# Half-row matmuls of the gate stage, side by side on the two halves of the array

## The chip, the cores and the metric

The kernel runs on one core of a Trainium2 chip. The metric is the device time of one launch in microseconds (us). The kernel before was run three times: 3077.47 us is the median, 3076.24 and 3080.39 us are the ends.

## The reference

Two layers on 2048 tokens of width 1024, then a final norm: an mLSTM layer, and a gated linear recurrence (RG-LRU). The change lies in the last stage, which does the second half of the RG-LRU layer. What is computed there:

```python
xc = causal_dwconv(xr, conv_w, conv_b)                      # 1536 channels
xb = xc.reshape(bsz, s, R_BLOCKS, R_BS)                     # 8 blocks of 192 channels
r  = sigmoid(einsum('bsnc,ncd->bsnd', xb, w_a).reshape(bsz, s, R_WIDTH) + b_a)
ig = sigmoid(einsum('bsnc,ncd->bsnd', xb, w_x).reshape(bsz, s, R_WIDTH) + b_x)
log_a = -LRU_C * r * softplus(-lam)
a  = exp(log_a)
bt = sqrt(-expm1(2.0 * log_a)) * (ig * xc)
hs = linear_scan(a, bt)                                     # h_t = a_t h_(t-1) + bt_t
y  = (hs * silu(g)) @ w_out                                 # 1536 -> 1024
x  = rmsnorm(x + y, final_g)
```

The two einsums are the gates: each is block diagonal, with blocks of 192 by 192.

## The kernel before, in words

The last stage is `phase_b2`. Channels lie on the 128 partitions, tokens on the free axis. Tokens go in four blocks `b` of 512, channels of the recurrence in four groups `p` of 384 = three tiles of 128 rows, which hold two of the 192-blocks: block one is tile 0 and rows 0 to 63 of tile 1, block two is rows 64 to 127 of tile 1 and tile 2. For each `b`, `p` and each of the two gates `j` (0 is `r`, 1 is `ig`), `gates` computes three output tiles `to`. Output tile 0 takes input tiles 0 and 1, output tile 1 takes 0, 1 and 2, output tile 2 takes 1 and 2: seven products. The weights are laid out as seven blocks of 128 by 128 in that order, with zeros where a product needs only half of the rows of tile 1 (the second and the sixth block).

Every product is done three times by `mm3` (lines 362 to 364): operands are split into a high part and a rest (`xch`, `xcl`, `wh`, `wl`; cast by ACT in line 735, rest by DVE in line 738), and high by high, high by rest and rest by high are summed in a bank of PSUM. So one gate of one group is 21 matmuls of 128 rows and 512 columns; there are 32 such sets. ACT then reads each bank: tanh, exp, tanh for `j` = 0 (lines 1298 to 1300, into `R` and `A`), one tanh for `j` = 1 (line 1302, into `ig`). A square root of `R` follows (line 1304), then the products and scans on DVE (lines 1307 to 1316), which give `yh` and `yl`.

`x2_out` multiplies these with the output weights (`acc`, 36 matmuls per step), adds the residual, and does the final norm (`ssum`, `srow`, `x2`, output). A list `steps` interleaves: one gate step, then, from the sixth gate step on, three steps of `x2_out` that lag five gate steps behind. The weights are fetched in that order, at most three ahead (`weights`, line 1242 for raw ones, which are split on the core; in block 0 the gates' split weights are also stored to DRAM, and blocks 1 to 3 load them back, line 1239). The order of instructions on each engine is made by a list scheduler from priorities and estimated times, so a change of one engine's order can change that of the others.

PE is TensorE; PEld are its weight loads, which have rows of their own in the trace; DVE, ACT, SP are VectorE, ScalarE, SyncE.

Of the kernel before, what the change touches and what calls it, by code (L numbers as in the profile page):

```python
# [14 lines left out]
P = 128  # L15
# [273 lines left out]
class Trunk:  # L289
# [923 lines left out]
    def phase_b2(self, rgate, rwout, D, outT):  # L1213


        tc, nc = self.tc, self.nc
        NT = 12
        with ExitStack() as ctx:
# [31 lines left out]
            def weights():  # L1250

                with tc.high_priority():
                    while order and len(ready) < 3:
                        ready.append(fetch(*order.pop(0)))
                return ready.pop(0)

            def psum(name):
                return pm.tile([P, TB], F32, tag="mm", name=name)

            def col(i, t):  # L1260
                return self.lc[:, i * NT + t:i * NT + t + 1]
# [19 lines left out]
            def gates(b, p, xs, ys):  # L1281

                R = tp.tile([P, 3, TB], F32, tag="R", name="R")
                A = tp.tile([P, 3, TB], F32, tag="A", name="A")
                G = tp.tile([P, 3, TB], F32, tag="ig", name="ig", bufs=1)
                xc, xh, xl = xs
                for j in range(2):
                    wh, wl = weights()
                    i = 0
                    for to, tis in ((0, (0, 1)), (1, (0, 1, 2)), (2, (1, 2))):  # L1290
                        ps = psum("gate")
                        for ti in tis:
                            ws = slice(i * P, (i + 1) * P)
                            self.mm3(ps, wh[:, ws], wl[:, ws], xh[:, ti], xl[:, ti], ti == tis[0], ti == tis[-1])
                            i += 1
                        t = p * 3 + to
                        if j == 0:
                            nc.scalar.activation(R[:, to], ps, AF.Tanh, scale=0.5, bias=col(2, t))
                            nc.scalar.activation(A[:, to], R[:, to], AF.Exp, scale=col(0, t), bias=col(0, t))
                            nc.scalar.activation(R[:, to], R[:, to], AF.Tanh, scale=col(1, t), bias=col(1, t))  # L1300
                        else:
                            nc.scalar.activation(G[:, to], ps, AF.Tanh, scale=0.5, bias=col(3, t))
                    if j == 0:
                        nc.scalar.activation(R, R, AF.Sqrt, scale=-0.25)
                        g = tp.tile([P, 3, TB], F32, tag="g", name="g")
                        nc.sync.dma_start(g, D["g"][p * 3:p * 3 + 3, :, b * TB:(b + 1) * TB].rearrange("k p t -> p k t"))
                        nc.vector.scalar_tensor_tensor(R, A, 1.0, R, op0=ALU.add, op1=ALU.mult)
                        yield
                nc.vector.scalar_tensor_tensor(xc, G, 1.0, xc, op0=ALU.add, op1=ALU.mult)
                nc.vector.tensor_tensor(R, R, xc, op=ALU.mult)  # L1310
                for to in range(3):
                    t = p * 3 + to
                    nc.vector.tensor_tensor_scan(xc[:, to], A[:, to], R[:, to], hc[:, t:t + 1], op0=ALU.mult,
                                                 op1=ALU.add)
                nc.gpsimd.tensor_copy(hc[:, p * 3:p * 3 + 3], xc[:, :, TB - 1])
                nc.vector.tensor_tensor(g, xc, g, op=ALU.mult)
                hi = tp.tile([P, 3, TB], F32R, tag="yh", name="yh", bufs=4)
                lo = tp.tile([P, 3, TB], F32R, tag="yl", name="yl", bufs=4)
                self.split_into(hi, lo, g, "a", "v")
                ys += [(hi[:, to], lo[:, to]) for to in range(3)]  # L1320
                yield

            def block(b):

                ys = blocks[b] = []
                if b == 0:
                    with tc.high_priority():
                        xs = load(b, 0)
                else:
                    xs = load(b, 0)  # L1330
                for p in range(4):
                    nxt = load(b, p + 1) if p < 3 else None
                    yield from gates(b, p, xs, ys)
                    xs = nxt
# [158 lines left out]
```

## Time and profile before

| | |
|---|---|
| median of 3 runs | 3077.47 us (3076.24 to 3080.39) |
| profiled execution | 3070.89 us, of which the span is 3069.1 us |
| PE busy | 2935.0 us, 96% |
| DVE, ACT busy | 2129.9 us (69%), 1460.0 us (48%) |
| last stage | from about 2584 us to the end |

The span runs from the first to the last instruction; what lies around it is 1.8 us. A matmul's row in the trace gives a time from start to end, but matmuls are pipelined: what one costs in a dense stream is the distance from its start to the next start, not its length.

### The profile page before, as it was taken

What the parts mean: (1) busy time and instruction counts of PE and PEld (TensorE: products, weight loads), DVE (VectorE), ACT (ScalarE), POOL (GpSimd) and SP (SyncE); (2) the same over time, 40 slices, a digit from 0 to 9 for tenths busy, and PEclk for the clock granted to TensorE, in tenths of its full rate; (3) what the DMA queues carried; (4) which work ended last, traced back from release to release, by engine and by line L of the source; (5) the groups of instructions that cost most, each with busy time, mean ns of one, the idle gap of its engine ahead of it and who ended that gap; (6) DMA issues with size and microseconds to landing.
All of it is one profiled execution on the core that took longest, in us unless ns stands there. A gap on an engine that the chain in (4) does not pass through costs nothing.

```text
span 3069.1 us, 43651 instructions
## 1 busy us (share of the span) xinstructions
PE 2935.0 (96%) x15730; PEld 2511.8 (82%) x15730; DVE 2129.9 (69%) x3825; ACT 1460.0 (48%) x2386; POOL 381.3 (12%) x407
## 2 busy tenths in 40 slices
PE   6999999999999899999999899999999998899997
PEld 4799987899988898989989777877888886687786
DVE  7866789534566587777778655687779375887775
ACT  5444546323434555555555322343445233877772
POOL 0111110000000234343333100000110000110100
PEclk9999999999999999999999899999999998999999
DMA  6766677666777645354534565666666666757743
GB/s 217 254 216 232 231 249 247 201 201 208 218 227 231 185 129 164 121 166 127 159 121 124 189 189 169 188 197 214 219 216 223 213 192 215 252 184 240 239 135 127
DMA packets 308986, 600.64 MB, mean 196 GB/s; under 512 B 27808, under 2 KB 106400, under 8 KB 308768
## 3 DMA queue, kind: packets, MB, share of 16 engines
q1 hardware_dynamic: 222784, 389.79, 41.6%
q10 hardware_dynamic: 59184, 107.77, 10.0%
q0 software_dynamic: 26800, 100.28, 8.4%
q8 instruction: 124, 2.03, 0.3%
q14 instruction: 94, 0.77, 0.1%
HBM read 388.86 MB, written 208.86 MB: 195 GB/s over the span
## 4 chain that ended last, share of the span: by engine, by line
PE 85%; DVE 6%; DMA 5%; ACT 2%; issue 1%; POOL 0%; SPq 0%; ACTq 0%; DVEq 0%; POOLq 0%
PE acc L362 6%; PE acc L363 6%; PE acc L364 6%; PE pj L362 3%; PE pj L363 3%; PE pj L364 3%; PE pd L362 3%; PE pc L362 3%; PE pd L363 3%; PE pd L364 3%; PE pc L364 3%; PE pc L363 3%; PE pa L362 3%; PE pa L363 3%; PE pa L364 3%; PE pb L363 2%
## 5 line engine op out<-in xcount | busy, mean ns | idle before, releaser
L735 ACT CAST s<-raw 128x512 fp32r<-128x512 f32 (+1 forms) x360 | 222.2, 621 | 500.9 <-PE acc L364 193.4
L738 DVE TENSOR_TENSOR s<-raw,s 128x512 fp32r<-128x512 f32 (+1 forms) x360 | 246.6, 688 | 91.5 <-ACT s L735 87.2
L362 PE MATMUL acc<-yh,s 128*128 128x512 f32 x512 | 204.5, 402 | 9.9 <-DVE x L1125 3.6
L363 PE MATMUL acc<-yl,s 128*128 128x512 f32 x512 | 203.9, 398 | 0.3 <-DVE yl L738 0.3
L364 PE MATMUL acc<-yh,s 128*128 128x512 f32 x512 | 202.8, 396 | 0.0
L362 PE MATMUL acc<-yh,wh 128*128 128x512 f32 x384 | 149.7, 397 | 13.5 <-ACT yh L735 8.9
L735 ACT CAST Ch<-C 128x516 fp32r<-128x516 f32 x120 | 74.8, 623 | 171.1 <-DVE da L944 120.1
L364 PE MATMUL acc<-yh,wl 128*128 128x512 f32 x384 | 150.9, 395 | 1.1 <-DVE wl L738 1.1
L363 PE MATMUL acc<-yl,wh 128*128 128x512 f32 x384 | 151.0, 394 | 0.3 <-DVE yl L738 0.2
L662 DVE SCALAR_TENSOR_TENSOR xc<-xm,vec,xc 128x512 f32<-128x512 f32 x192 | 140.3, 746 | 14.5 <-ACT xc L660 13.4
L735 ACT CAST s<-sum 128x512 fp32r<-128x512 f32 (+1 forms) x120 | 74.3, 620 | 146.7 <-PE pa L364 43.6
L738 DVE TENSOR_TENSOR Cl<-C,Ch 128x516 fp32r<-128x516 f32 x120 | 116.7, 972 | 20.9 <-ACT Ch L735 20.7
L362 PEld LDWEIGHTS acc<-yh,s 128*128 128x128 f32 x512 | 97.8, 191 | 35.7 <-DVE x L1125 4.5
L364 PEld LDWEIGHTS acc<-yh,s 128*128 128x128 f32 x512 | 97.3, 190 | 23.2 <-DVE s L738 0.3
L363 PEld LDWEIGHTS acc<-yl,s 128*128 128x128 f32 x512 | 97.3, 190 | 22.9 <-DVE yl L738 0.8
L735 ACT CAST wh<-wr 128x512 fp32r<-128x512 f32 (+1 forms) x104 | 65.4, 641 | 102.1 <-PE acc L363 63.6
L662 DVE SCALAR_TENSOR_TENSOR xc<-xr,vec,xc 128x512 f32<-128x512 f32 x144 | 104.8, 747 | 7.3 <-ACT xc L660 6.0
L738 DVE TENSOR_TENSOR s<-sum,s 128x512 fp32r<-128x512 f32 (+1 forms) x120 | 82.4, 688 | 39.2 <-ACT s L735 38.1
L738 DVE TENSOR_TENSOR wl<-wr,wh 128x512 fp32r<-128x512 f32 (+1 forms) x104 | 73.4, 716 | 51.7 <-ACT wh L735 51.2
L362 PE MATMUL gate<-xch,wh 128*128 128x512 f32 x224 | 92.7, 415 | 16.7 <-ACT xch L735 8.8
L362 PE MATMUL pj<-vwh,xmh 128*128 128x512 f32 x256 | 103.4, 404 | 0.0
L364 PE MATMUL pj<-vwh,xml 128*128 128x512 f32 x256 | 100.5, 392 | 0.0
(419 smaller groups left out, 9684.9 us busy)
## 6 DMA issues: line engine op xcount, KB each, us to landing
d_wx<-s POOLq DMA_DIRECT2D x64, 512.0 KB, 4.1
s<-d_wx SPq DMA_DIRECT2D x64, 512.0 KB, 4.4
raw<-in_wout_dram SPq DMA_DIRECT2D x128, 256.0 KB, 3.1
raw<-in_wxz_dram SPq DMA_DIRECT2D x124, 256.0 KB, 4.5
d_wr<-s POOLq DMA_DIRECT2D x48, 512.0 KB, 3.4
s<-d_wr SPq DMA_DIRECT2D x48, 512.0 KB, 4.4
wr<-in_rwout_dram SPq DMA_DIRECT2D x96, 256.0 KB, 2.9
raw<-in_rwin_dram SPq DMA_DIRECT2D x84, 256.0 KB, 3.8
```

What stands on the lines that cost most here:

```text
L362: mm(out, sh, mh, start=first, stop=False, skip_group_check=resumed)
L363: mm(out, sh, ml, start=False, stop=False, skip_group_check=resumed)
L364: mm(out, sl, mh, start=False, stop=last, skip_group_check=resumed)
L662: nc.vector.scalar_tensor_tensor(out, x[:, j:j + TB], self.v(wn, m * 4 + j), out, op0=ALU.mult, op1=ALU.add)
L735: a = nc.scalar.copy(hi, src)
L738: b = (nc.gpsimd if lo_eng == "p" else nc.vector).tensor_tensor(lo, src, hi.bitcast(F32), op=ALU.subtract)
```

## The change

Two of the seven products, output tile 0 with input tile 1 and output tile 2 with input tile 1, are issued on the 64 rows that are not zero: rows 0 to 63 for the one, rows 64 to 127 for the other. Their three parts are issued in turn, one for each of the two banks: six matmuls of 64 rows and 512 columns. For this the two banks are opened first with the whole products of tiles 0 and 2, and output tile 1 comes last, in matmuls as before. ACT reads the banks in the order 0, 2, 1. The number of matmuls per set stays 21.

```diff
-                    i = 0
-                    for to, tis in ((0, (0, 1)), (1, (0, 1, 2)), (2, (1, 2))):
-                        ps = psum("gate")
+                    pss = {}
+
+                    def full(to, tis, n, first, last):
                         for ti in tis:
-                            ws = slice(i * P, (i + 1) * P)
-                            self.mm3(ps, wh[:, ws], wl[:, ws], xh[:, ti], xl[:, ti], ti == tis[0], ti == tis[-1])
-                            i += 1
+                            ws = slice(n * P, (n + 1) * P)
+                            self.mm3(pss[to], wh[:, ws], wl[:, ws], xh[:, ti], xl[:, ti], first and ti == tis[0],
+                                     last and ti == tis[-1])
+                            n += 1
+                    for to, n in ((0, 0), (2, 6)):
+                        pss[to] = psum("gate")
+                        full(to, (to,), n, True, False)
+
+                    ends = ((0, slice(0, 64), slice(P, 2 * P)), (2, slice(64, P), slice(5 * P, 6 * P)))
+                    for st, mv in ((wh, xh), (wh, xl), (wl, xh)):
+                        for to, rs, ws in ends:
+                            nc.tensor.matmul(pss[to], st[rs, ws], mv[rs, 1], start=False, stop=st is wl)
+                    pss[1] = psum("gate")
+                    full(1, (0, 1, 2), 2, True, True)
+                    for to in (0, 2, 1):
+                        ps = pss[to]
                         t = p * 3 + to
```

On PE, in a set of the dense middle of the stage, this stands before around the product of output tile 0 with input tile 1 (`gate_27284` is the bank of output tile 0, `gate_27292` that of tile 1; the shape at the end is that of the output):

```order
L364 MATMUL gate_27284<-xch_26948,wl_27245 128x512
L362 MATMUL gate_27284<-xch_26948,wh_27244 128x512
L363 MATMUL gate_27284<-xcl_26949,wh_27244 128x512
L364 MATMUL gate_27284<-xch_26948,wl_27245 128x512
L362 MATMUL gate_27292<-xch_26948,wh_27244 128x512
L363 MATMUL gate_27292<-xcl_26949,wh_27244 128x512
```

The second to the fourth row are that product; bank after bank is finished. The same place in the changed kernel (`gate_27284` output tile 0, `gate_27288` tile 2, `gate_27298` tile 1; line 1304 is the new matmul):

```order
L364 MATMUL gate_27284<-xch_26948,wl_27245 128x512
L362 MATMUL gate_27288<-xch_26948,wh_27244 128x512
L363 MATMUL gate_27288<-xcl_26949,wh_27244 128x512
L364 MATMUL gate_27288<-xch_26948,wl_27245 128x512
L1304 MATMUL gate_27284<-xch_26948,wh_27244 128x512
L1304 MATMUL gate_27288<-xch_26948,wh_27244 128x512
L1304 MATMUL gate_27284<-xcl_26949,wh_27244 128x512
L1304 MATMUL gate_27288<-xcl_26949,wh_27244 128x512
L1304 MATMUL gate_27284<-xch_26948,wl_27245 128x512
L1304 MATMUL gate_27288<-xch_26948,wl_27245 128x512
L362 MATMUL gate_27298<-xch_26948,wh_27244 128x512
```

The six of line 1304 stand together, banks in turn, between matmuls of 128 rows; in 30 of the 32 sets it is so, in the other two they are in two pieces (three and three, one and five).

On ACT, at the start of the stage (first group, first gate; the 896-wide cast is that of the next gate's weights), the difference begins so:

```order
 L735 CAST xch<-xc 128x512
-L1298 ACTIVATE R<-gate,lc 128x512
+L1311 ACTIVATE R<-gate,lc 128x512
+L1312 ACT_TABLE_LOAD
+L1312 ACTIVATE A<-R,lc 128x512
 L735 CAST wh<-wr 128x896
-L1299 ACT_TABLE_LOAD
-L1299 ACTIVATE A<-R,lc 128x512
 L735 CAST xch<-xc 128x1536
```

A table load and the exp have moved ahead of the weights' cast.

## Rows read from the trace of the kernel before

**Rows 1.** The page: span, and PE's busy time, share and instructions
```profile
span 3069.1 us, 43651 instructions
PE 2935.0 (96%) x15730; PEld 2511.8 (82%) x15730; DVE 2129.9 (69%) x3825; ACT 1460.0 (48%) x2386; POOL 381.3 (12%) x407
```

**Rows 2.** Stretches: us, busy us (x) of PE PEld DVE ACT POOL, PEclk, DMA share, GB/s
```profile
2590.00:2620.00 30.00, 22.04 (x73) 16.29 (x72) 12.34 (x10) 21.93 (x27) 3.24 (x6) 0.83 0.97 358
...
2700.00:2750.00 50.00, 50.00 (x220) 41.04 (x219) 39.08 (x37) 38.92 (x50) 5.40 (x2) 1.00 0.56 191
```

**Rows 3.** Chain that ended last, last stage: start us, us, what
```profile
2688.44 0.24 PE acc L364
...
2769.25 0.89 PE srow L1029 x8
...
2797.47 1.71 PE acc L362 x4
...
2897.39 0.24 PE gate L364
...
2909.01 1.20 PE acc L362 x4
...
3004.53 0.24 PE acc L363
```

**Rows 4.** Timeline of a dense set: start us, us, engine, line, operation
```profile
2690.12 0.39 PE L363 MATMUL acc<-yl,wh 128*128 128x512 f32 x1
2690.12 0.19 PEld L364 LDWEIGHTS acc<-yh,wl 128*128 128x128 f32 x1
...
2702.94 0.39 PE L362 MATMUL gate<-xch,wh 128*128 128x512 f32 x1
...
2707.75 0.39 PE L362 MATMUL acc<-yh,wh 128*128 128x512 f32 x1
```

**Rows 5.** Timeline around one matmul on 64 rows, first stage
```profile
922.48 0.39 PE L364 MATMUL pd<-t1h,s 128*128 128x512 f32 x1
...
922.80 0.14 PEld L726 LDWEIGHTS st<-ident,gate 64*128 64x128 f32 x1 [0.36 <-issue]
922.80 0.27 PE L726 MATMUL st<-ident,gate 64*128 64x64 f32 x1
...
923.00 0.50 PE L362 MATMUL pa<-u11h,s 128*128 128x512 f32 x1
...
923.34 0.39 PE L363 MATMUL pa<-u11l,s 128*128 128x512 f32 x1
```

**Rows 6.** Timeline around four matmuls on 64 rows, first stage
```profile
924.74 0.39 PE L363 MATMUL pa<-u11l,s 128*128 128x512 f32 x1
925.06 0.33 PE L726 MATMUL st<-ident,gate 64*128 64x64 f32 x2
925.24 0.38 PE L727 MATMUL st<-ident,gate 64*128 64x64 f32 x2
925.55 0.50 PE L364 MATMUL pa<-u11h,s 128*128 128x512 f32 x1
925.89 0.39 PE L362 MATMUL pa<-u21h,s 128*128 128x512 f32 x1
```

**Rows 7.** Timeline where matmuls have few columns
```profile
300.01 0.28 PE L362 MATMUL oa<-s,u21h 128*128 128x258 f32 x1
300.13 0.28 PE L363 MATMUL oa<-s,u21h 128*128 128x258 f32 x1
...
2755.13 0.95 PE L1019 MATMUL ssum<-ones,sacc 128*128 128x1 f32 x8
...
2755.93 0.48 PE L362 MATMUL gate<-xch,wh 128*128 128x512 f32 x1
```

**Rows 8.** Timeline of ACT at the start of the last stage
```profile
2593.89 0.68 ACT L1298 ACTIVATE R<-gate,lc 128x512 f32<-128x512 f32 x1
2595.32 0.94 ACT L735 CAST wh<-wr 128x896 fp32r<-128x896 f32 x1 [0.76 <-DMA wr<-in_rgate_dram]
2596.28 1.28 ACT L1299 ACT_TABLE_LOAD   x1
```

## The prediction

> **What bounds the kernel now.** I read the page first: PE is busy 96% of a span of 3069.1 us [rows 1]. An average over stages doesn't say what the last stage is worth, so I read the stretches next. From 2590 to 2620 us PE is busy only 22 of 30 us and the DMA engines 0.97 of theirs: the stage begins bound by loads. From 2700 to 2750 us PE is busy all of 50 us at a granted clock of 1.00, that is 2.4 GHz, while DVE has 39 and ACT 39 [rows 2]. The chain says where PE's time reaches the end: it runs on PE from 2688.44 to 2769.25, from 2797.47 to 2897.39 and from 2909.01 to 3004.53 us [rows 3]; between these it runs through DMA, ACT and DVE until `yh` is ready and PE's `acc` goes on. The three stretches are 80.8, 99.9 and 95.5 us, together 276 us. So a us saved or added on PE counts in these, a us saved elsewhere becomes a wait.
>
> How many sets of gate matmuls lie there? The set at 2702.94 us ends where `acc` starts at 2707.75: 21 matmuls in 4.81 us, 0.229 us from start to start [rows 4]. The row's 0.39 us is a length in a pipeline and no price. A set with its 36 `acc` matmuls is 57 x 0.229 = 13.05 us, and 276 / 13.05 = 21 sets. Of the 32 sets (four blocks, four groups, two gates) five or six lie in the start, bound by loads, and the rest in the gaps of the chain.
>
> **The change part by part.** *What is removed.* No matmul: six of 21 change their shape, from 128 rows to 64, at the same 512 columns. A dense matmul's time goes by its columns (0.12 us apart at 258 of them [rows 7], 0.229 at 512), so a half-row matmul alone saves nothing; the only gain there can be is two of them running at once, on different rows. At best six pitches become three: 3 x 0.229 = 0.69 us per set.
>
> *What is added: two switches per set*, from 128-row to 64-row matmuls and back. The trace has no 512-column matmul on 64 rows, but it has the switch, in the first stage. A dense 128-row matmul starts at 922.48 us; the weight load of the 64-row one starts at 922.80, with nothing else waited for ("issue"), 0.32 us later and not beside its predecessor. In a dense stream a load does start with the matmul before it: both rows at 2690.12 us [rows 4]. Behind the 64-row matmul the next 128-row one starts at 923.00, its length 0.50 instead of 0.39 and its successor 0.34 us on instead of 0.229: 0.11 us of weight load lies bare ahead of its stream [rows 5]. From 922.48 to 923.34 are 0.86 us where two pitches would be 0.46, so one small matmul with both switches costs 0.40 us. Four of them: 924.74 to 925.89 is 1.15, less 0.46 is 0.69 us [rows 6]. Three more cost 0.29, so about 0.10 each, and some 0.30 us is the price of the two switches themselves. Of the 0.20 us from 922.80 to 923.00 the small matmul's own load and its 64 columns take about 0.11, so about 0.09 is emptying before the way back.
>
> *The loads.* Six half-row matmuls need six weight loads of 128 columns. Each of the matmuls of 258 columns, 0.12 us apart, has its own load, and eight matmuls of one column take 0.80 us with theirs, 0.10 each [rows 7]; with the bare 0.11 of the switch [rows 5] I take 0.11, bounds 0.10 and 0.12. At 0.229 us per pair, two loads of 0.11 just fit.
>
> *The sum for a set*, from the start of the last 128-row matmul ahead of the six to the start proper of the first one behind. Before: 7 x 0.229 = 1.60 us. After: 0.32 to the first load; six loads one behind another, 6 x 0.11 = 0.66; the last half matmul's stream, 0.23; emptying 0.09; a bare load 0.11: together 1.41 us (1.35 to 1.47). That is 0.19 us less, bounds 0.13 and 0.25. Over 21 sets: 4.0 us, bounds 2.7 and 5.3. In this each half matmul starts when its load is done, and the two row halves overlap by about half their streams.
>
> *What is moved.* Output tile 1 now ends the set and banks 0 and 2 are ready together. ACT then has its three activations of one tile after PE's last matmul, as before; in the dense stretches ACT has 11 of 50 us free [rows 2], and PE has `acc` to do meanwhile, so I cost it at nothing. If that cover is gone it is one tile's tanh, some 0.7 us, at each place where PE waits for `yh`, of which there are four: up to 2.7 us. At the start the order on ACT puts a table load and an exp ahead of the cast of the second gate's weights. That cast ran at 2595.32, released by its load, 0.75 us after the tanh's end at 2594.57; now 1.28 for the table and about 0.7 for the exp come first, and the cast stands at about 2596.6, 1.3 us later [rows 8]. Behind it, through one raw buffer, waits the next load of gate weights on SP's queue, and behind that the stage's start. With the DMA engines at 0.97 the delayed load finds less company, so the loss is 0 to 1.3 us; I take the middle, 0.7. SP's queue issues one load of `g` and two of `x` earlier, the same bytes in the same busy stretch: nothing, give or take 1 us.
>
> Together: -4.0 + 0.7 = -3.3 us. The profiled execution, 3070.89 us (span and 1.8 us around it), would come to 3067.6. The median of the runs lies 6.6 us above that execution; I take the difference over to it: 3077.47 - 3.3 = 3074.2 us. Its own range: 2.7 to 5.3 less, 0 to 1.3 more, 1 either way, so 3071 to 3077.
>
> **Rivals.**
>
> *No overlap (slower).* The half-row matmuls run one behind another at 0.229 us, only with their loads hidden: 0.32 + 0.11 + 6 x 0.229 + 0.09 + 0.11 = 2.00 us against 1.60, 0.40 us more per set. PE's additions count outside the 21 sets too, since the chain's gaps hold waits of PE of 2 to 4 us only: 21 to 27 sets, 8.4 to 10.8 us, with the start 3087.8 us. For it: no row of the trace shows two matmuls at once, and the 64-row ones there lie all on the same rows. Against: they differ in rows and in banks, and nothing else is shared that a row shows to be full. It decides the sign from the point where less than about a third of a stream is overlapped (the 0.40 us must be earned back over five overlaps of 0.08).
>
> *Whole pairs.* Both halves load and run side by side, so a pair takes one pitch: 0.32 + 0.11 + 3 x 0.229 + 0.09 + 0.11 = 1.32 us, 0.28 less per set, 5.9 us over 21 sets, 3072.3 us with the start. Against it: all loads in the trace follow one another on one queue, 0.10 to 0.12 us apart [rows 7]. The Trainium skill ("TensorE: Matmul & The Clock Gate", "Measured speedup vs the span model") gives a pack of row tiles the time of one matmul plus about 4 ns per further tile, which is this case; no run so far shows it here.
>
> *Loads that wait for their own rows.* If a half's next load must wait until the matmul on those rows is through, a pair costs 0.229 + 0.11 = 0.34 us: 0.11 + 2 x 0.34 + 0.11 + 0.23 = 1.13 in place of 0.89, 1.65 us per set, 0.05 more than before. That is 1 us more over 21 sets, 3079.2 us with the start: no change. Against it: the load and the matmul at 2690.12 us share all 128 rows and start together [rows 4]. The same page of the Trainium skill ("The mechanism") says that a load overlaps a running matmul only where the row group differs; the rows at 2690.12 us contradict it for the whole array, and for 64 rows no row decides.
>
> *A free switch.* If the tolls [rows 5, 6] belong to those small matmuls and not to the change of rows, 0.69 us per set is kept: 14.5 us, 3063 us. Against it, both places pay it in the same size.
>
> **How the numbers follow.** The forecast has 0.37, no overlap 0.26, whole pairs 0.20, waiting loads 0.12, the free switch 0.05. A measurement of this kernel tells about 0.2%, 6.2 us, from no change; the bounds are 3071.3 and 3083.6. Faster: 0.15 of the forecast's 0.37 (a better start), 0.4 of the pairs' 0.20, and the free switch: 0.06 + 0.08 + 0.05 = 0.19. Slower: nearly all of no overlap, 0.23, and 0.02 from the others, 0.25. The rest, 0.56, is within. The range runs from 3067 to 3088 us: it takes in the forecast, the pairs, the waiting loads and over half of no overlap, and leaves out the free switch and the upper part of no overlap.
>
> **What would show it.** In the timeline of the changed kernel, the six rows of line 1304: starts about 0.11 us apart show the forecast, pairs of starts that lie together 0.23 apart show whole pairs, 0.23 from each to the next no overlap. The first load of the six 0.32 us behind the last 128-row matmul's start, and a first 128-row matmul of 0.50 us behind them, show the tolls. A dense set, now 4.81 us, should take 4.6. The cast of the second gate's weights should start about 1.3 us later than the row at 2595.32. Wrong would be: a set of 5.2 us or of 4.1, or PE waiting over 4 us for `yh` at the block boundaries, where the time would come from ACT's new order.

## The result, and the profile after

The changed kernel takes 3085.38 us (median of 8 runs, 3082.8 to 3090.22) against 3077.48 us (8 runs, 3070.57 to 3080.58). The ratio is 1.0031, 95% interval 1.0021 to 1.0042: it is slower, by 7.9 us in the medians and by about 9.5 us by the ratio (0.0031 x 3077). Forecast were 3074.2 us. The profiled execution of after took 3085.59 us, near its median; that of before lay 6.6 us under its own, so the two profiles differ by 14.6 us of span, some 5 to 7 us more than the runs do. What follows from single profiles is uncertain by as much.

The page of after, against [rows 1]:

```profile
span 3083.7 us, 43658 instructions
...
PE 2934.7 (95%) x15730; PEld 2493.5 (81%) x15730; DVE 2130.5 (69%) x3825; ACT 1457.4 (47%) x2386; POOL 372.6 (12%) x407
```

PE is busy as long as before, 2934.7 us. Its weight loads fell by 18 us, so the pairs did something.

**The set itself did better than forecast.** PE in a dense set of after (start us, us, engine, line, operation; x2 is two records told as one row):

```profile
2723.26 0.40 PE L364 MATMUL gate<-xch,wl 128*128 128x512 f32 x1
2723.59 0.50 PE L1304 MATMUL gate<-xch,wh 64*128 64x512 f32 x2
2723.92 0.39 PE L1304 MATMUL gate<-xcl,wh 64*128 64x512 f32 x2
2724.15 0.40 PE L1304 MATMUL gate<-xch,wl 64*128 64x512 f32 x2
2724.48 0.50 PE L362 MATMUL gate<-xch,wh 128*128 128x512 f32 x1
2724.82 0.39 PE L363 MATMUL gate<-xcl,wh 128*128 128x512 f32 x1
```

The loads of the same six, and of the first matmul behind them:

```profile
2723.59 0.18 PEld L1304 LDWEIGHTS gate<-xch,wh 64*128 64x128 f32 x2 [0.36 <-issue]
2723.69 0.19 PEld L1304 LDWEIGHTS gate<-xcl,wh 64*128 64x128 f32 x2
2723.93 0.19 PEld L1304 LDWEIGHTS gate<-xch,wl 64*128 64x128 f32 x2
2724.48 0.19 PEld L362 LDWEIGHTS gate<-xch,wh 128*128 128x128 f32 x1 [0.36 <-issue]
```

Two half-row matmuls together take 0.18 us for their loads and 0.23 us to the next pair: both halves load and run side by side. The tolls for the change of rows are those of [rows 5]: 0.33 us from 2723.26 to the first load, and at 2724.48 a bare load, 0.50 long and 0.34 to its successor. From 2723.26 to 2724.48 and 0.11 of bare load are 1.33 us where seven pitches were 1.60: 0.27 us less a set. A set with its 36 `acc` matmuls repeats every 12.78 us, where it was 13.05.

**The stage lost more than that.** I cut the last stage at each block's first `srow` on PE. Columns are us, then the busy us of the engines, PEclk (the granted clock as a share of 2.4 GHz), DMA share and GB/s. Before:

```profile
2583.90:2769.10 185.20, 167.36 (x684) 132.51 (x685) 137.83 (x132) 144.40 (x179) 26.13 (x21) 0.95 0.69 240
2769.10:2882.10 113.00, 109.25 (x473) 88.80 (x472) 86.94 (x96) 79.99 (x103) 10.95 (x4) 0.98 0.64 216
2882.10:2990.80 108.70, 106.48 (x473) 87.30 (x472) 85.16 (x94) 77.17 (x100) 8.83 (x4) 1.00 0.56 188
2990.80:3058.10 67.30, 60.30 (x263) 47.40 (x261) 39.18 (x58) 19.89 (x31) 1.71 (x1) 0.97 0.34 114
```

After:

```profile
2583.80:2774.20 190.40, 166.41 (x684) 122.71 (x685) 138.18 (x132) 141.15 (x177) 18.92 (x21) 0.92 0.67 230
2774.20:2888.00 113.80, 108.10 (x475) 83.73 (x474) 86.85 (x95) 78.24 (x101) 8.82 (x4) 0.97 0.63 213
2888.00:3000.90 112.90, 107.73 (x474) 83.02 (x473) 85.39 (x94) 77.12 (x101) 9.28 (x4) 0.97 0.55 185
3000.90:3072.90 72.00, 61.19 (x263) 48.21 (x261) 38.98 (x58) 22.96 (x33) 2.17 (x1) 0.94 0.34 110
```

The four parts take 5.2, 0.8, 4.2 and 4.7 us longer. No engine has clearly more work; PE waits more, and its granted clock is lower in every part. What PE waited for in the whole last stage (line and tile, releaser: us in total, times, longest), before:

```profile
PE acc L362 <- ACT yh L735: 8.9, 4, 3.8
PE gate L362 <- ACT xch L735: 8.8, 2, 5.0
PE gate L362 <- ACT wh L735: 4.9, 2, 2.6
...
PE acc L362 <- ACT wh L735: 2.4, 3, 1.4
```

After:

```profile
PE gate L362 <- ACT xch L735: 10.9, 2, 5.9
PE gate L362 <- ACT wh L735: 8.7, 4, 2.9
PE acc L362 <- ACT yh L735: 8.1, 4, 2.8
PE acc L362 <- ACT wh L735: 6.1, 2, 5.6
PE gate L362 <- ACT ig L1315: 4.1, 2, 2.6
...
PE gate L363 <- DVE xcl L738: 2.9, 1, 2.9
```

All rows of this view together are 35.0 us before and 50.0 after: 15.0 more, as much as the stage grew (14.7). By part of the stage the waits rose from 21.9 to 28.4 up to the first `srow`, from 3.8 to 5.8 and from 2.2 to 5.2 in the two blocks behind it, from 7.1 to 10.6 at the end. The 32 sets' gain of 0.27 us (8.6 us) isn't seen in PE's busy time, since more of that time passes at the lower level of the granted clock, 1.2 GHz: 42.4 us of the last stage, where it was 24.7 before. Half of such time is lost, 8.8 us more than before.

ACT's order around the first boundary between blocks has changed too. Before (start us, us; in brackets ACT's own idle time ahead of the row and what ended it):

```profile
2761.29 1.49 ACT L735 CAST yh<-g 128x1536 fp32r<-128x1536 f32 x1 [0.72 <-DVE g L1316]
...
2768.16 1.49 ACT L1304 ACTIVATE R<-R 128x1536 f32<-128x1536 f32 x1
...
2770.59 0.58 ACT L1382 COPY rb<-srow 128x512 f32<-128x512 f32 x1
...
2782.85 0.62 ACT L735 CAST wh<-wr 128x512 fp32r<-128x512 f32 x1 [4.27 <-DMA out_dram<-x]
...
2795.95 1.47 ACT L735 CAST yh<-g 128x1536 fp32r<-128x1536 f32 x1 [1.86 <-DVE g L1316]
```

After:

```profile
2763.82 1.26 ACT L1311 ACTIVATE R<-gate,lc 128x512 f32<-128x512 f32 x2 [2.80 <-PE gate L1304]
...
2769.10 1.48 ACT L735 CAST yh<-g 128x1536 fp32r<-128x1536 f32 x1 [2.60 <-DVE g L1329]
...
2776.61 1.49 ACT L1317 ACTIVATE R<-R 128x1536 f32<-128x1536 f32 x1
...
2778.52 0.57 ACT L1395 COPY rb<-srow 128x512 f32<-128x512 f32 x1
...
2789.76 0.62 ACT L735 CAST wh<-wr 128x512 fp32r<-128x512 f32 x1 [5.52 <-DMA out_dram<-x]
...
2804.51 1.47 ACT L735 CAST yh<-g 128x1536 fp32r<-128x1536 f32 x1 [2.05 <-DVE g L1329]
```

Measured from `srow` on the chain (2769.25 in [rows 3], 2774.30 in after), the square root starts 1.1 us ahead of it before and 2.3 behind it after; the copy of the norm's row follows 1.3 and 4.2 behind, and the `yh` with which PE goes on 26.7 and 30.2. ACT takes its work in the order of its list: it now waits 2.80 us for the pairs' banks, then 2.60 us at a `yh` cast whose input DVE hasn't finished, and work that is ready stands behind (PE ends output tile 1 at 2766.05, its tanh starts at 2772.42). The square root is 3.4 us late and the gap 3.5 us longer. That the one makes the other is not shown: the chain that ended last goes another way here. Before, it goes from the norm's products through an output store on ACT's queue to `ig`:

```profile
2775.33 7.07 DMA out_dram<-x
```

In after it goes through an output store and the load of `x` behind it, at all three boundaries; at the first:

```profile
2782.51 6.70 DMA out_dram<-x
...
2790.16 5.53 DMA x<-d_x
```

### The profile page after: what moved, and what is told of

Read it like the earlier page. It is cut to its first block, busy times and chain, and to the rows that moved or that the text cites. A ratio compares the mean times of both kernels' runs of the same rounds, so it can differ in the third digit from the quotient of the medians.

```text
span 3083.7 us, 43658 instructions
## 1 busy us (share of the span) xinstructions
PE 2934.7 (95%) x15730; PEld 2493.5 (81%) x15730; DVE 2130.5 (69%) x3825; ACT 1457.4 (47%) x2386; POOL 372.6 (12%) x407
## 4 chain that ended last, share of the span: by engine, by line
PE 86%; DVE 5%; DMA 5%; ACT 2%; issue 1%; POOL 0%; SPq 0%; ACTq 0%; DVEq 0%; POOLq 0%
PE acc L362 6%; PE acc L363 6%; PE acc L364 6%; PE pj L362 3%; PE pj L363 3%; PE pj L364 3%; PE pd L362 3%; PE pd L363 3%; PE pc L362 3%; PE pd L364 3%; PE pc L364 3%; PE pc L363 3%; PE pa L362 3%; PE pa L363 3%; PE pa L364 3%; PE pb L363 2%
## 5 line engine op out<-in xcount | busy, mean ns | idle before, releaser
L362 PEld LDWEIGHTS acc<-yh,wh 128*128 128x128 f32 x384 | 74.4, 195 | 38.8 <-ACT yh L735 9.9
```

The lines of the kernel that those rows point to most:

```text
L362: mm(out, sh, mh, start=first, stop=False, skip_group_check=resumed)
```

## The experiments

Each was timed beside runs of the kernel before on the same chip; the ratio is to that kernel, and the interval behind it is its 95% interval. "Last stage" is from the first `xch` cast to the end of one profiled execution (before 485.2 us, after 499.9).

**Same order, whole rows.** The six keep their place, and the order on each engine is that of after; they use 128 rows.

```diff
-ends = ((0, slice(0, 64), slice(P, 2 * P)), (2, slice(64, P), slice(5 * P, 6 * P)))
+ends = ((0, slice(0, P), slice(P, 2 * P)), (2, slice(0, P), slice(5 * P, 6 * P)))
```

> Every instruction stands on every engine where it stands in the changed kernel; only the six matmuls of a set use 128 rows again (the other 64 are zeros in the weights), so no two run at once and no switch is left. Theory O (the order that came with the change costs the time, the half rows themselves gain): a dense set goes from 12.78 us back to 13.05 us with its acc matmuls, 0.27 us in about 21 sets, so about 5.7 us slower than the changed kernel, near 3091 us. Rival P (the half rows themselves cost it, by switches outside the dense stretches or by a lower clock): the time returns to that of the kernel before, near 3077 us.

3082.24 us, ratio 1.0031 [1.0019, 1.0044], the same as after (the two theories had named 3091 and 3077). So the loss is the order's, not the half rows', and of what the pairs save on PE nothing is seen in the time; the two intervals leave room for 0.16%, some 5 us, either way. PE's waits are 46.1 us instead of 50.0, the last stage 498.6. Its parts behind the first `srow`:

```profile
2772.10:2886.70 114.60, 110.36 (x473) 89.14 (x472) 86.97 (x95) 78.36 (x101) 8.82 (x4) 0.97 0.62 210
2886.70:3002.00 115.30, 110.45 (x473) 88.56 (x472) 86.09 (x95) 78.40 (x102) 9.28 (x4) 0.99 0.54 182
3002.00:3069.20 67.20, 59.53 (x263) 47.49 (x261) 38.20 (x57) 20.74 (x31) 2.17 (x1) 0.97 0.34 114
```

With pairs the first two were 0.8 and 2.4 us shorter and the last 4.8 longer: PE waited 5.6 us for `wh` there, and here 1.8. So in these two executions the pairs do shorten the middle blocks, and the last part takes it back. Over the whole last stage the pairs spare PE 9.2 us, counted at the full clock; 6.7 come back because PE is busy for 42.4 us at 1.2 GHz instead of 29.0, and 3.9 as waits.

**Both halves on the same rows.** Both slices are 0 to 63, so output tile 2 leaves out rows 64 to 127 of input tile 1.

> The order of the changed kernel, but both products take rows 0 to 63 (output tile 2 is then computed from the wrong half of tile 1). Two matmuls can't run on the same rows at once, the switches stay. If the gain in the dense sets is the running side by side, the six take 0.33 + 0.11 + 6 x 0.229 + 0.09 + 0.11 = 2.0 us in place of 1.33: 0.67 us more per set, 14 to 18 us over 21 to 27 sets, near 3101 us. If the six are cheap for another reason (64 rows being quicker), it takes no more than the changed kernel, 3085 us.

The set, in PE's timeline:

```profile
2745.90 0.39 PE L364 MATMUL gate<-xch,wl 128*128 128x512 f32 x1
2746.22 0.73 PE L1304 MATMUL gate<-xch,wh 64*128 64x512 f32 x2
2746.79 0.62 PE L1304 MATMUL gate<-xcl,wh 64*128 64x512 f32 x2
2747.25 0.62 PE L1304 MATMUL gate<-xch,wl 64*128 64x512 f32 x2
2747.80 0.50 PE L362 MATMUL gate<-xch,wh 128*128 128x512 f32 x1
```

On the same rows two matmuls take 0.46 us, one behind the other; 1.90 and 0.11 are 2.01 us a set, 0.68 more than in after and 21.8 us over 32 sets. The time is 3083.44 us, ratio 1.0033 [1.0022, 1.0045]: of the 21.8 us no more than some 5 can be there by the intervals. PE's waits fall to 33.9 us, 16.1 less than in after, and its busy time at 1.2 GHz to 28.5. Sets of 1.33, 1.60 and 2.01 us in one order give one time within these 5 us: in this order PE's time in a set is for the most part hidden.

**Pairs first.** The six open the set, then outputs 0, 1 and 2 end in that order.

```diff
-                        full(to, (to,), n, True, False)
...
+                    for i, (st, mv) in enumerate(((wh, xh), (wh, xl), (wl, xh))):
...
+                            nc.tensor.matmul(pss[to], st[rs, ws], mv[rs, 1], start=i == 0, stop=False)
+                    for to, tis, n in ((0, (0,), 0), (1, (0, 1, 2), 2), (2, (2,), 6)):
...
```

> The six half-row matmuls open the set (they start both banks), then output tiles 0, 1, 2 follow as in the kernel before, so ACT gets its banks in the order 0, 1, 2. Theory O: the gain of the pairs (0.27 us in 21 sets, 5.7 us) is kept, and the 13 us that the profiles show as lost at the start and at the block boundaries come back for the most part: 3072 us, faster than the kernel before. Rival P: as slow as the changed kernel, 3085 us. If any new order costs about as much as this one did: between 3077 and 3085.

3079.28 us, 1.0020 [1.0011, 1.0029], in the third of the ranges named. The stage up to the first `srow` is back at 185.4 us (before 185.2, after 190.4), but the two blocks behind it take 115.3 and 115.5. So in this execution the loss lies at the boundaries and not at the start. The start differs between executions, too: among all profiled kernels, two with the order of before up to the first `srow` took 185.2 and 188.7 us, four with that of after 189.5 to 190.8.

**The change from block 1 on**, block 0 as before.

> Blocks 1 to 3 as in the changed kernel, block 0 as in the kernel before. In the profiles the dense part starts 7 us later in the changed kernel (2693.1 against 2686.1 us), and the three block boundaries lose 3.5 to 4.5 us each. If the start is a loss of its own, this kernel is about 7 us faster than the changed one but for the 1 to 2 us that the pairs gain in block 0: near 3080 us. If the loss lies at the boundaries alone, 3085 to 3087 us.

3080.9 us, 1.0022 [1.0012, 1.0032], near the 3080 expected for a start that is a loss of its own; but against 1.0031 the intervals overlap. Most of the loss stays without the change at the start.

**Stores from POOL's queue** in blocks 0 to 2, for before, after and pairs first. In after ACT stood 5.52 us at a cast behind its own queue's stores.

```diff
-(nc.scalar if m % 2 or not last else nc.sync).dma_start(outT[m, :, bs], x2[m])
+(nc.gpsimd if not last else nc.scalar if m % 2 else nc.sync).dma_start(outT[m, :, bs], x2[m])
```

> The kernel before, with the outputs of blocks 0 to 2 stored from POOL's queue instead of ACT's. In the kernel before, ACT goes from the norm's factor (rb, 1.1 to 1.5 us behind srow) through eight stores, two of its pieces stalled behind the stores, to the next ig only 13 to 14 us behind srow, and yh, for which PE waits, is cast 25 to 27 us behind srow. Theory O (ACT's order at the block boundary sets the gap): ig comes some 8 us earlier, the gap shrinks until PE's own 99 matmuls in it (23 us) bound it, 2 to 4 us at each of three boundaries, so 6 to 11 us faster than the kernel before. Rival P (the gap is set by PE or the loads): no change.

> The same with the changed kernel. Theory O: the three gaps, 29 to 32 us from srow to yh, shrink to PE's own work of some 22 us, and the gain of the dense sets shows: only the loss at the start (about 4 us, as the spans of the start in three kernels of this order against two of the other) stays. About 15 to 20 us faster than the changed kernel, and within 3 us of the kernel before with the same stores. Rival P: 3085 us as before.

> The half-row pairs at the head of the set, outputs in the order 0, 1, 2, and the stores from POOL's queue. Theory O: no loss at the start (105.6 us to the first dense part in the kernel with pairs first, against 104 to 107 before), gaps bound by PE, and 0.27 us less in some 27 sets that now count: about 6 us faster than the kernel before with the same stores, 12 to 17 us faster than the kernel before. Rival P: as the kernel before with the same stores.

Before with it: 3067.18 us, 0.998 [0.997, 0.9991]. After: 3077.09, 1.0012 [1.0003, 1.0021]. Pairs first: 3077.24, 1.0009 [1.0, 1.0018]. It helps before and after by 0.2% each, pairs first by 0.1% (where the intervals overlap). The changed kernel, expected within 3 us of before with the same stores, stays 0.32% behind it, and pairs first, expected 6 us ahead, 0.29%: the stores aren't what tells them apart.

**The norm at high priority** (`srow`, its copy, the products and the stores) in after.

```diff
-                rb = self.stats_rows(pm, rc, "mm")
...
+                with tc.high_priority():
+                    rb = self.stats_rows(pm, rc, "mm")
...
```

> The changed kernel with the norm's last part (srow, rb, the scaling and the stores) at a higher priority for the list scheduler: on ACT rb then stands ahead of the last tanh and the square root of the gate in front of it, instead of behind. Stores stay on ACT's queue. If rb's place behind the square root is what lengthens the gap (rb 4.4 to 4.6 us behind srow instead of 1.1 to 1.5), it comes back to about 1.3 us and each gap is some 3 us shorter: 8 to 10 us faster than the changed kernel, near 3076 us. If the stores' stall alone sets the gap, it moves with them and the time stays at 3085 us, or the stalled stores now delay the gate's tanh and it is slower.

3077.98 us, 1.0011 [1.0, 1.0022]. The copy stands 1.2 to 2.1 us behind `srow` again, and the ratio is two thirds of the loss lower; the gap up to the next `yh` is still 32 to 35 us, and the square root now stands 14 to 20 us behind `srow`. The kernel before was not run with this edit, so it isn't shown that the edit puts right what the change spoiled.

**The gates at high priority**: tanh, exp and square root of blocks 1 to 3, in after, and with the stores from POOL in pairs first and in before.

```diff
+                        with tc.high_priority() if b else ExitStack():
+                            if j == 0:
+                                nc.scalar.activation(R[:, to], ps, AF.Tanh, scale=0.5, bias=col(2, t))
...
```

> The changed kernel with ACT's activations of the gates (and the square root) in blocks 1 to 3 at a higher priority for the list scheduler; nothing is taken away. At the block boundary ACT then finishes the three tanh and exp ahead of the cast of yh, the square root no longer stands behind a weight cast that waits for PE, and the three ig stand ahead of the stores. The start has the changed kernel's order. Theory O: the square root comes at or ahead of srow again (2.5 to 2.8 us behind it in the changed kernel), ig some 10 us earlier, the gaps shrink from 30 us to 25 or less, and with the pairs' 0.27 us per set the time is some 12 to 18 us below the changed kernel: 3064 to 3070 us, under the kernel before in spite of the start. Rival P: 3085 us.

> Pairs at the head of the set, stores from POOL's queue, and the gates' activations of blocks 1 to 3 at the higher priority. In the same kernel without the priority the square root stood 2.4 to 2.8 us behind srow and PE waited 4.6 to 5.0 us at a boundary for yh. Theory O: the square root comes ahead of srow, yh 18 to 20 us behind it as in the kernel before with these stores, PE waits under 2 us, and the pairs' gain shows: some 6 us below the kernel before with these stores (3067 us), 3060 to 3063 us. If it stays at 3077 us, the place of the square root isn't the cause.

> The kernel before with the stores from POOL's queue and the same priority, without pairs: what the two edits give by themselves. Its square root stood ahead of srow already (0.9 to 1.1 us), so theory O expects no more than 2 us from the priority: 3065 to 3068 us, some 5 us above the same with pairs.

After: 3074.16 us, 0.9992 [0.9982, 1.0002]. Pairs first with both edits: 3066.58, 0.9966 [0.9952, 0.9979]. Before with both: 3058.85, 0.9947 [0.993, 0.9963], better than I had expected and the lowest ratio of all, without any pairs. Of the three expectations none was met: after came 4 us above its range, pairs first with both 4 above, before with both 6 below.

The first of these looks as if ACT's order had been put right; that needs its control. It also says something of the square root. In after with the gates first, `srow` is at 2772.57, and on ACT stand

```profile
2771.53 1.49 ACT L1319 ACTIVATE R<-R 128x1536 f32<-128x1536 f32 x1
...
2804.00 1.47 ACT L735 CAST yh<-g 128x1536 fp32r<-128x1536 f32 x1
```

The square root is 1.0 us ahead of `srow` again, and the copy 1.4 behind, as before; but the next `yh` still comes 31.4 us behind `srow`, and this block takes 113.1 us where after took 113.8. So the late square root alone is not what makes the block long.

**Controls**: before with the gates' priority alone; after with both edits; pairs first with both edits and whole rows (the same order on every engine).

> The kernel before with the gates' activations and the square root at high priority in blocks 1 to 3, and nothing else; stores stay on ACT's queue. It is the control for the same edit in the changed kernel, which came out 0.08% under the kernel before. Theory one, that this edit only puts right what the change spoiled on ACT: the kernel before gains nothing from it, 0.9990 to 1.0010 of it. Theory two, that the edit is worth about 8 us (0.27%) in any order, as it was on top of the stores from POOL's queue: 0.9965 to 0.9980, and then the changed kernel still loses some 0.2% against its control.

> The changed kernel with both edits: stores of blocks 0 to 2 from POOL's queue, and gate activations and square root at high priority in blocks 1 to 3. Its control is the kernel before with the same two, at 0.9947 of the kernel before. If ACT's order and the stores were all that ate the gain, the pairs now show: 0.9925 to 0.9945. If the later start and the gates' later results (outputs 0 and 2 both end behind output 1's row of products) cost by themselves, it stays at 0.9960 to 0.9975.

> Pairs first with both edits (0.9966 of the kernel before), but the six products on all 128 rows, every engine's order being the same. If PE's time in the dense stretches is hidden behind ACT and DVE here too, the time is the same to 0.1%: 0.9956 to 0.9976. If the pairs now count, 21 sets give back up to 0.28 us each, 5.9 us: 0.9975 to 0.9990.

Before with the gates' priority: 3062.34 us, 0.9962 [0.9949, 0.9976], just below theory two's range. So the edit is worth as much without the change (0.38% against 0.39%), and repairs nothing that the change spoiled. After with both: 3062.87, 0.9957 [0.9944, 0.997], between the two ranges that I had given. Whole rows: 3066.36, 0.9971 [0.996, 0.9983], in the first of its ranges, where the pairs had 0.9966: they are 0.05% apart, give or take 0.18%, so the 32 x 0.27 = 8.6 us (0.28%) of the pairs aren't there in full. The ratios side by side:

| | plain | stores from POOL | gates first | both |
|---|---|---|---|---|
| before | 1 | 0.9980 | 0.9962 | 0.9947 |
| after | 1.0031 | 1.0012 | 0.9992 | 0.9957 |
| difference | 0.31% | 0.32% | 0.30% | 0.10% |

Either edit alone leaves the loss as it is. With both it is 0.10%, give or take 0.2%: neither that a rest is left nor, strictly, that it shrank is shown. In the last two columns the two runs come from different chips. The windows of one block (the second `srow` from the first) show what happens in it. Before with both edits:

```profile
2766.30:2872.60 106.30, 106.30 (x473) 87.33 (x472) 86.18 (x96) 79.31 (x102) 17.38 (x12) 1.00 0.66 228
```

After with both:

```profile
2769.40:2875.40 106.00, 104.39 (x473) 81.66 (x473) 85.88 (x95) 77.45 (x102) 13.59 (x12) 1.00 0.65 228
```

Pairs first with both, and the same with whole rows:

```profile
2776.30:2884.40 108.10, 106.44 (x473) 82.70 (x472) 86.30 (x95) 78.53 (x102) 17.99 (x12) 0.98 0.65 224
```

```profile
2772.20:2880.00 107.80, 106.73 (x474) 87.37 (x473) 86.35 (x95) 78.52 (x102) 18.00 (x12) 1.00 0.65 225
```

In the first PE is busy for all of 106.30 us at a granted clock of 1.00, with no wait: this is a block bound by PE. With the pairs (after with both) it has 1.9 us less to do and waits 1.6 us for a weights' cast on ACT, so the block is 0.3 us shorter. In pairs first PE waits 1.7 us for `yh` and 1.1 with whole rows, and behind the longer wait its granted clock is lower, 0.98 of 1.00 over the block: it reaches the wait sooner and leaves it slower.

## Why the prediction was wrong

The step that failed: "a us saved or added on PE counts in these" dense stretches, and with it "so I cost it at nothing" for ACT's order. Each dense stretch ends in a boundary where PE waits for ACT and DVE. A us saved in the stretch brings PE to that wait a us sooner; it counts only if what PE waits for comes sooner as well. It doesn't: from `srow` (its first row in PE's timeline) to the next `yh` the three gaps are 30.4, 29.4 and 31.6 us with pairs, 29.4, 30.0 and 26.0 with whole rows, 28.5, 28.1 and 25.0 with both halves on the same rows, and 26.9, 25.3 and 25.2 in the kernel before. One order with sets of 1.33, 1.60 and 2.01 us gave 1.0031, 1.0031 and 1.0033. The saving of the pairs came back as waits and as work at 1.2 GHz, and the order that came with them cost 0.31%.

Forecast were 3.3 us less, measured 7.9 us more. The time does lie in the range that I gave, 3067 to 3088 us, but by luck: its upper part stood for half-row matmuls that do not overlap, and these overlap in full.

- *Switches*: 0.32 and 0.11 us forecast, 0.33 and 0.11 measured.
- *Loads*: one behind another at 0.11 was wrong; the loads of the two halves go side by side too. The set is that of *Whole pairs*, 1.33 us for 1.32, and saves 0.27 us where 0.19 were forecast. The rule of the Trainium skill ("TensorE: Matmul & The Clock Gate", "Measured speedup vs the span model") that was weighed there holds in this trace: a pair takes 0.23 us as one whole matmul did. The other rule of that page ("The mechanism"), that a load overlaps a running matmul only where the row group differs, doesn't; the same section also has loads into a background weight buffer pulled ahead, and these rows fit that. The second pair's loads start at 2723.69, while the first pair is on the same rows, and on the same rows two matmuls with their loads take 0.46 us, two pitches and no more.
- *Sum over 21 sets*: 5.7 us was there to be had by that step; the run with whole rows in the same order has the same ratio, so nothing of it is seen (within some 5 us).
- *ACT's order*: priced at nothing, at most 2.7 us. Its rows of PE's waits (`xch`, `wh`, `yh`, `ig`, `R`) went from 30.1 to 43.2 us. I had looked at ACT's free share (11 of 50 us in [rows 2]), an average over the dense middle; at the boundary it is the order that counts, and there I hadn't followed where the `yh` cast and the square root come to stand.
- *Start*: the cast of the second gate weights was forecast at about 2596.6 and stands at 2596.49; but the loss isn't 0.7. By the seventh cast of gate weights the lag has grown from 1.2 to 2.3 us (2636.09 to 2638.39), by the eighth and last to 4.4 (2642.61 to 2647.00), and PE waits 7.2 us more up to the first dense stretch (19.8 to 27.0, rows of PE's waits up to 2684 and 2691 us). In pairs first 5.0 of the 5.2 us up to the first `srow` are back; executions of one order differ there by up to 3.5 us.
- *The sign I had named* was "PE waiting over 4 us for `yh`": the longest is 2.8, shorter than the 3.8 before. The waits moved to `wh`, `ig` and `xch`, and to the last block, where one for `wh` takes 5.6 us. Of the cause named beside it, ACT's new order, it is shown that the order decided, and not that ACT's part of it did.

Shown are that the order costs 0.31% and the half rows nothing that could be told (0.16%), that the pairs' gain is for the most part hidden in this order, and where PE waits. Open is what in the order costs it. The square root's lateness does not suffice: with the gates first it stood ahead of `srow` again and the block stayed as long to 0.7 us. The norm moved forward gave back two thirds of the loss, but the kernel before never had that edit. Open is also whether an order exists in which pairs shorten a block that PE fills without waiting; pairs first was the only other order tried.

## What to carry to other kernels

Before a saving on the busiest engine is counted, follow its stretch to the wait in which it ends: the saving is worth what the releaser of that wait also gains. Where one list orders all engines, a change of one engine's order must be priced on the others by reading their new order at the boundaries, and tested by a twin that keeps the order and drops the saving. An edit that wins back a loss proves nothing until the kernel before has had the same edit: here the kernel before with both side edits, 3058.85 us, has the lowest time of all; no version with pairs is faster.

## What was not expected of the hardware

- Two matmuls of 64 rows and 512 columns on different halves of the array, each with its own weights and into its own bank, take 0.23 us a pair, loads included (0.18 us for two loads); on the same half they take 0.46.
- The toll for leaving and regaining 128 rows is the same for 512 columns as for the 64 columns of [rows 5]: 0.33 us to the first load, and a bare load of 0.11 us behind.
- Stores issued from ACT's queue held ACT's own work up to 5.52 us (a cast of weights, in after); with the stores on POOL's queue the kernel before is 0.2% faster.
- A wait costs more than its length: behind the 5.6 us for `wh` in after, PE's granted clock is 0.50, that is 1.2 GHz, from 3019.6 to 3026.4 us, and its `acc` matmuls are 0.43 us apart instead of 0.23.
